# A hybrid encoder step on one core: new order of the last output tiles, of the first loads, and of everything a planner places between them

## The chip, the cores and the metric

The kernel runs on 1 core of one Trainium2 chip. The metric is the device time of one execution in microseconds (us). The time before is the median of three runs.

## The reference, cut to what matters

One layer of a streaming encoder, for 512 rows of a prompt and 32 rows of a sample (544 rows together) of width 1024. All arithmetic is float32.

```python
z = _rmsnorm(x, g) @ w_in                       # 3880 columns, split into the inputs of three groups of heads
oa = band attention (group A, 6 heads x 64)     # own chunk and the 8 before it, relative-position bias
ob = sparse attention (group B, 6 heads x 64)   # an indexer (8 heads x 32, one key) picks the best keys of each row
om = attention into 256 memory rows (group M, 4 heads x 64)
o = jnp.concatenate([oa * jax.nn.silu(ga), ob * jax.nn.silu(gb), om * jax.nn.silu(gm)], axis=-1)
x = x + o @ w_out                               # 1024 x 1024
y = _rmsnorm(x, norm_final_g)                   # the final norm
```

The keys and values of all groups are outputs too; the sample rows attend into caches of 512 (A), 1024 (B) and 256 (M) rows as well.

## The kernel before

**Products.** Each float32 operand is split into a high and a low part (names with h and l: wh, wl, xTh, xTl, oBh, oBl). A product of two operands is three matmuls (wh with xTh, wl with xTh, wh with xTl) that add up in one PSUM bank. For weights, ACT makes wh from the raw columns and POOL or DVE makes wl = raw - wh; for x, ACT makes xTh and DVE makes xTl.

**Order.** Nothing is ordered by hand. All instructions are recorded by one helper (so nearly all rows of the trace have line L400). A planner, the class Line, keeps an estimated clock for each engine and for the DMA queue of SP; generators (one for each task, such as loading, splitting, attention, output) yield the estimated time at which they want to go on, and the planner lets the one go on that fits. What a DMA is taken to last is a rate in `op` (L249). A generator that needs a PSUM bank waits in `room` or asks `there` (L458 to 472) until the bank is, by the estimate, free for some margin. So the numbers in these places decide the order in which every engine gets its instructions:

```python
        d = (outs[0].size() * 4 / 330e3 if eng == "SP" else
             self.cost(eng, op, outs, ins, kw) * (1.0 if eng == "PE" else SLACK))
            t = sorted(pp.free(f"b{b}") for b in free_banks)[k - 1] + 0.7
```

**Start.** `x_load` (L800) issues on SP's queue the norm weights g_mix, and for each of 8 K tiles (128 rows of the 1024) the K tile of x transposed (xr, 128 x 544) and the 296 columns of w_in for the indexer (raw, 128 x 296). ACT and DVE split both, and `index_group` multiplies: 8 K tiles, for each three token tiles of 128 rows, for each three matmuls of 296 columns, that is 72 matmuls. When PE's clock is behind the time at which operands are estimated to be there, `warm` (L909) puts filler matmuls `idle<-ones` into the gap (float32, so each is two passes and counts as two in the trace), with LATER = 0.3 us added to the gap.

**Middle.** Projections of all other columns with weights in pieces of 128 x 384 to 768; the three attentions; the sample's attention, with matmuls on parts of the array (forms 128\*64, 128\*32, 64\*128 in the trace); the caches of the sample are loaded by SP.

**End.** The output projection, `out_part` (L1963), is done in two parts: the heads of A and part of M first, and the rest (list B: three heads pairs of B and one tile of M) last. Part B before goes through columns 0 to 511 for token tiles t0 to t3 and then through columns 512 to 1023 for t0 to t3, the last in two halves of 256. Each result is added to the rows of x (`residual`, tile xr), and `settle` makes the final norm: a sum of squares of each piece (ACT, the last piece on DVE), the adds of these sums (tile ss, on POOL), the power -1/2 (POOL), the products with that factor and with norm_final_g (gf; on ACT, POOL, DVE), and a DMA of the whole 128 x 1024 tile out.

Of the kernel before, what the change touches and what calls it, by code (L numbers as in the profile page):

```python
# [91 lines left out]
class Line:  # L92
# [139 lines left out]
    def op(self, eng, op, outs, ins, kw):  # L232
# [11 lines left out]
        for x in outs_:  # L244
            b = self.box(x)
            for (w, _), o in self.reads[x.tensor.name].items():
                if all(p[0] < q[1] and q[0] < p[1] for p, q in zip(w, b)):
                    deps.setdefault(o, False)
        d = (outs[0].size() * 4 / 330e3 if eng == "SP" else  # L249
             self.cost(eng, op, outs, ins, kw) * (1.0 if eng == "PE" else SLACK))  # L250
# [178 lines left out]
def hybrid_step(ctx: ExitStack, tc: tile.TileContext, a: dict):  # L429
# [28 lines left out]
    def room(k=1):  # L458

        yield from line.wait(lambda: len(free_banks) >= k)  # L460
        while True:
            t = sorted(pp.free(f"b{b}") for b in free_banks)[k - 1] + 0.7
            if t <= line.now():
                return
            yield t
            yield from line.wait(lambda: len(free_banks) >= k)
# [4 lines left out]
    def there(k):  # L471
        return k == 0 or len(free_banks) >= k and sorted(pp.free(f"b{b}") for b in free_banks)[k - 1] + 0.7 <= line.now()

# [326 lines left out]
    def x_load():  # L800

        c = len(x_raw)
        yield from ()
        t = (rp.tile([P, 2, N], F32, tag="xr", name="xr", bufs=3) if c < 3 else
             cp.tile([P, 2, N], F32, tag="gate1", name="xr"))
        if c % 2 == 0:
            firsts.append(cp.tile([P, 2, 2, 296], F32, tag=("q0", "gate0")[c // 2], name="raw"))
        raw = firsts[c // 2][:, c % 2]
        for kk in range(2):
            rows = slice((2 * c + kk) * P, (2 * c + kk + 1) * P)  # L810
            if c == kk == 0:
                DMA.dma_start(gT[0], a["norm_mix_g"])
            DMA.dma_start(t[:, kk, :], a["x_t"][rows, :])
            DMA.dma_start(raw[:, kk, :], w_in[rows, QI:QI + 296])
        raws.append(raw)
        x_raw.append(t)
# [92 lines left out]
    def warm(until):  # L909
        fill, line.warm = line.warm, None  # L910
        until += LATER if until - line.clk["PE"] > WARM else 0
        while until - line.clk["PE"] > WARM:
            PE.matmul(idle[:, 0:P], ones, ones, start=True, stop=True)
        line.warm = fill
# [1048 lines left out]
    def out_part(ks, c0, done, order, apart=()):  # L1963

        ws = []
        for t in order:
            halves = 2 if t in apart else 1
            n = 512 // halves
            for f0 in range(0, 512, n):
# [3 lines left out]
                for i, k in enumerate(ks):  # L1973
                    if i == len(ws):
                        ws.append(w_next(1 + i))
                    wh, wl = (w[:, 0, f0:f0 + n] for w in ws[i])
                    st, en = i == 0, i == len(ks) - 1
# [7 lines left out]
                    PE.matmul(o, h, wl, start=False, stop=en)  # L1985
                line.spawn(evict([acc], [1], lambda _, p, t=t, f0=f0, n=n: residual(t, p[:, 0:n], c0 + f0, n),
                                 lambda t=t, f0=f0, n=n: done(t, c0 + f0, n)))

    def residual(t, acc, c0, n):
        x = xr[t][:, c0:c0 + n]  # L1990
        V.tensor_tensor(x, acc[:, 0:n], x, op=ALU.add)

    for c0 in range(0, D, 512):
        line.run(out_part(AM, c0, lambda *_: None, range(NT)))

# [14 lines left out]
    line.spawn(final())  # L2010
    pieces = [0] * (NT + 1)

    def settle(t, c0, n):
# [6 lines left out]
        new, run, old = s_[:, 2 * j:2 * j + 1], s_[:, 2 * j + 1:2 * j + 2], s_[:, 2 * j - 1:2 * j]  # L2020
        last = t == NT - 1 and c0 + n == D
        yield line.at(x) - 0.2
        if last:
            V.tensor_tensor_reduce(sq[:rows, 0:n], in0=x, in1=x, scale=1.0 / D, scalar=0.0, op0=ALU.mult, op1=ALU.add,
                                   accum_out=new)
        else:
            A.activation(sq[:rows, 0:n], x, AF.Square, scale=D ** -0.5, accum_out=new)
        if j == 0 or t == NT - 2:
            G.tensor_tensor(x, x, gf[:rows, c0:c0 + n], op=ALU.mult)
        yield line.at(new) - 0.2  # L2030
        if c0 + n < D:
            if j == 0:
                V.tensor_scalar(run, new, EPS, None, op0=ALU.add)
            else:
                G.tensor_tensor(run, new, old, op=ALU.add)
            return
        G.tensor_tensor(run, new, old, op=ALU.add)
        G.tensor_tensor(run, run, nhalf[:rows], op=ALU.pow)
        yield line.at(run) - 0.2
        y = xr[t]  # L2040

        m = D if t == NT - 2 else 512
        A.activation(y[:rows, 0:m], y[:rows, 0:m], AF.Copy, scale=run)
        if m < D:
            V.scalar_tensor_tensor(y[:rows, m:D], y[:rows, m:D], run, gf[:rows, m:D], op0=ALU.mult, op1=ALU.mult)
        DMA.dma_start(a["y_prompt"][t * P:(t + 1) * P, :] if t < NT else a["y_sample"], y)

    for c0 in range(0, D, 512):
        line.run(out_part(B, c0, lambda t, c, n: line.spawn(settle(t, c, n)),
                          range(NT), (NT - 1,) if c0 else ()))  # L2050
    while line.tasks:
# [66 lines left out]
```

## Time and profile before

| what | us |
|---|---|
| median of 3 runs | 354.46 |
| the three runs | 354.28, 354.46, 355.96 |
| the profiled execution, own time | 354.01 |
| its span (first to last instruction) | 352.2 |
| PE busy | 343.6 (98% of the span) |
| DVE, ACT, POOL busy | 278.3, 221.2, 179.5 |

The span is what the trace shows; the execution's own time is 1.8 us more. Busy time is the union of an engine's instructions: matmuls overlap, so the start of one to the start of the next says what one costs.

### The profile page before, as it was taken

The page shows a single profiled execution, that of the slowest core. Times are in us where ns is not written, and L with a number is a line of the kernel's source. Part 1 is how long each engine was busy: PE and PEld are TensorE (multiplying, and loading weights), DVE is VectorE, ACT ScalarE, POOL GpSimd, SP SyncE. Part 2 cuts the span into 40 slices and gives each one's busy share as a digit, 9 for nine tenths or more (in the row PEclk, how much of TensorE's full clock was granted, in tenths as well). Part 3 has the DMA queues.
Part 4 walks back from the last instruction along what each step waited for, and adds up shares of the span by engine and source line. Part 5 has one row for each costly group of instructions (what it writes and reads, how often), then busy time and mean ns, then how long its engine had stood idle before and what let it go on. Part 6 is the DMA issues. An engine that isn't in the chain of part 4 may idle for free.

```text
span 352.2 us, 7548 instructions
## 1 busy us (share of the span) xinstructions
PE 343.6 (98%) x2744; PEld 299.6 (85%) x2744; DVE 278.3 (79%) x705; ACT 221.2 (63%) x528; POOL 179.5 (51%) x197
## 2 busy tenths in 40 slices
PE   8999999999999999999999999999999999999991
PEld 7979978999999988887998998999986767776781
DVE  3765988878999979998999727999996689776552
ACT  5756677997767776786765328414793368573453
POOL 2568094475475557274654484552382064316543
PEclk9999999999999999999999999999999999999997
DMA  7999352375548223252131341234273285200014
GB/s 234 308 372 355 98 180 61 106 203 150 149 128 292 62 62 112 56 154 86 47 91 45 92 144 42 56 87 145 63 293 128 64 271 186 81 2 2 0 54 200
DMA packets 39604, 46.31 MB, mean 131 GB/s; under 512 B 5360, under 2 KB 32624, under 8 KB 39568
## 3 DMA queue, kind: packets, MB, share of 16 engines
q1 hardware_dynamic: 39568, 45.85, 41.8%
q8 instruction: 21, 0.34, 0.4%
q14 instruction: 15, 0.12, 0.1%
HBM read 39.67 MB, written 6.16 MB: 130 GB/s over the span
## 4 chain that ended last, share of the span: by engine, by line
PE 95%; DMA 1%; POOL 1%; SPq 1%; DVE 1%; issue 0%; ACT 0%; POOLq 0%; DVEq 0%; ACTq 0%
PE bank L400 95%; DMA xr<-in_x_t_dram 1%; SPq L400 1%; DVE xr L400 0%; POOL xr L400 0%; POOL ss L400 0%; ACT sq L400 0%; POOLq L2106 0%; DVE wl L400 0%; DVEq L400 0%; ACTq L400 0%
## 5 line engine op out<-in xcount | busy, mean ns | idle before, releaser
L400 POOL TENSOR_TENSOR wl<-raw,wh 128x512 fp32r<-128x512 f32 (+1 forms) x69 | 105.4, 1537 | 80.0 <-ACT wh L400 73.9
L400 ACT ACTIVATE wh<-raw 128x512 fp32r<-128x512 f32 (+2 forms) x77 | 50.5, 660 | 31.6 <-PE bank L400 17.1
L400 PE MATMUL bank<-wh,xTh 128*128 128x384 f32 (+1 forms) x184 | 63.8, 347 | 0.0
L400 PE MATMUL bank<-wl,xTh 128*128 128x384 f32 (+1 forms) x184 | 61.8, 336 | 0.4 <-DVE wl L400 0.4
L400 PE MATMUL bank<-wh,xTl 128*128 128x384 f32 (+1 forms) x184 | 61.2, 332 | 0.0
L400 ACT ACTIVATE z<-z,st 128x384 f32<-128x384 f32 (+3 forms) x80 | 42.4, 549 | 22.9 <-DVE st L400 22.7
L400 PE MATMUL bank<-xTh,wh 128*128 128x272 f32 x208 | 46.1, 303 | 0.0
L400 PE MATMUL bank<-xTh,wl 128*128 128x272 f32 x208 | 43.0, 288 | 0.0
L400 PE MATMUL bank<-xTl,wh 128*128 128x272 f32 x208 | 42.9, 288 | 0.0
L400 PEld LDWEIGHTS bank<-wh,xTh 128*128 128x128 f32 x184 | 34.9, 189 | 2.7 <-issue 2.0
L400 PEld LDWEIGHTS bank<-wl,xTh 128*128 128x128 f32 x184 | 34.7, 189 | 1.0 <-DVE wl L400 0.7
L400 PEld LDWEIGHTS bank<-wh,xTl 128*128 128x128 f32 x184 | 34.8, 189 | 0.0
L400 PEld LDWEIGHTS bank<-xTh,wh 128*128 128x128 f32 x208 | 32.7, 189 | 2.0 <-issue 1.4
L400 PEld LDWEIGHTS bank<-xTl,wh 128*128 128x128 f32 x208 | 32.6, 188 | 0.0
L400 PEld LDWEIGHTS bank<-xTh,wl 128*128 128x128 f32 x208 | 32.5, 189 | 0.0
L400 DVE MAX8 m<-ysel 128x8 f32<-128x256 f32 (+2 forms) x48 | 26.4, 550 | 0.1
L400 DVE MATCH_REPLACE8 ysel<-m,ysel 128x256 f32<-128x256 f32 (+2 forms) x48 | 26.1, 543 | 0.0
L400 PE MATMUL bank<-ident,z 128*128 128x128 f32 (+1 forms) x162 | 25.2, 275 | 0.0
L400 PEld LDWEIGHTS bank<-ident,z 128*128 128x128 f32 (+1 forms) x162 | 18.5, 140 | 5.5 <-issue 2.5
L400 ACT ACTIVATE junkS<-ysS,bi 128x1056 int8<-128x1056 f32 x16 | 18.7, 1169 | 4.3 <-DVE bi L400 4.3
L400 ACT COPY z<-bank 128x384 f32<-128x384 f32 (+2 forms) x26 | 13.2, 511 | 9.6 <-PE bank L400 8.5
L400 POOL TENSOR_TENSOR oBl<-o,oBh 128x128 fp32r<-128x128 f32 (+1 forms) x9 | 5.2, 577 | 27.1 <-ACT oBh L400 27.1
(300 smaller groups left out, 803.9 us busy)
## 6 DMA issues: line engine op xcount, KB each, us to landing
raw<-in_w_in_dram SPq DMA_DIRECT2D x20, 384.0 KB, 3.4
raw<-in_w_in_dram SPq DMA_DIRECT2D x26, 256.0 KB, 3.0
raw<-in_w_out_dram SPq DMA_DIRECT2D x16, 256.0 KB, 3.9
xr<-in_x_t_dram SPq DMA_DIRECT2D x8, 272.0 KB, 4.4
nat<-in_x_prompt_dram SPq DMA_DIRECT2D x4, 512.0 KB, 8.1
raw<-in_w_mem_kv_dram SPq DMA_DIRECT2D x8, 256.0 KB, 2.9
xr<-in_x_prompt_dram SPq DMA_DIRECT2D x4, 512.0 KB, 3.4
out_dram<-xr SPq DMA_DIRECT2D x4, 512.0 KB, 2.6
```

The lines of the kernel that those rows point to most:

```text
L400: return fn(*args, **kw)
```

## The change

Four edits. (1) At the end, part B goes through t0, t1, t2 with columns 0 to 511, the same three with columns 512 to 1023, and then t3 with both, its last piece in two halves. The sum of squares of t3's last half is started from the sum so far (`scalar=old`, `accum_out=run`), so no add follows it; t2 is treated like t0 and t1, with only its columns 0 to 511 multiplied by gf on POOL. (2) At the start x's first K tile is issued ahead of g_mix, and from the second K tile on the index weights are issued ahead of x. (3) The planner takes a DMA's rate as 200e3 for the first 2.5 us of SP's clock and as 370e3 after, in place of 330e3, and a margin of 1.0 in place of 0.7 for banks. (4) `warm` adds LATER only up to 7.5 us of the estimate.

```diff
-        d = (outs[0].size() * 4 / 330e3 if eng == "SP" else
+        d = (outs[0].size() * 4 / (200e3 if self.clk["SP"] < 2.5 else 370e3) if eng == "SP" else
...
-            t = sorted(pp.free(f"b{b}") for b in free_banks)[k - 1] + 0.7
+            t = sorted(pp.free(f"b{b}") for b in free_banks)[k - 1] + 1.0
...
             if c == kk == 0:
+                DMA.dma_start(t[:, kk, :], a["x_t"][rows, :])
                 DMA.dma_start(gT[0], a["norm_mix_g"])
-            DMA.dma_start(t[:, kk, :], a["x_t"][rows, :])
             DMA.dma_start(raw[:, kk, :], w_in[rows, QI:QI + 296])
+            if c + kk > 0:
+                DMA.dma_start(t[:, kk, :], a["x_t"][rows, :])
...
-        until += LATER if until - line.clk["PE"] > WARM else 0
+        until += LATER if WARM < until - line.clk["PE"] and until < 7.5 else 0
...
-        last = t == NT - 1 and c0 + n == D
+        last = c0 + n == D
         yield line.at(x) - 0.2
-        if last:
-            V.tensor_tensor_reduce(sq[:rows, 0:n], in0=x, in1=x, scale=1.0 / D, scalar=0.0, op0=ALU.mult, op1=ALU.add,
-                                   accum_out=new)
+        if t == NT - 1 and last:
+
+            yield from line.wait(lambda: summed[t] == j)
+            V.tensor_tensor_reduce(sq[:rows, 0:n], in0=x, in1=x, scale=1.0 / D, scalar=old, op0=ALU.mult, op1=ALU.add,
+                                   accum_out=run)
         else:
             A.activation(sq[:rows, 0:n], x, AF.Square, scale=D ** -0.5, accum_out=new)
-        if j == 0 or t == NT - 2:
-            G.tensor_tensor(x, x, gf[:rows, c0:c0 + n], op=ALU.mult)
-        yield line.at(new) - 0.2
-        if c0 + n < D:
+            yield line.at(new) - 0.2
             if j == 0:
                 V.tensor_scalar(run, new, EPS, None, op0=ALU.add)
             else:
                 G.tensor_tensor(run, new, old, op=ALU.add)
+        summed[t] += 1
+        if j == 0:
+            G.tensor_tensor(x, x, gf[:rows, c0:c0 + n], op=ALU.mult)
+        if not last:
             return
-        G.tensor_tensor(run, new, old, op=ALU.add)
+        yield line.at(run) - 0.2
         G.tensor_tensor(run, run, nhalf[:rows], op=ALU.pow)
...
-        m = D if t == NT - 2 else 512
-        A.activation(y[:rows, 0:m], y[:rows, 0:m], AF.Copy, scale=run)
-        if m < D:
-            V.scalar_tensor_tensor(y[:rows, m:D], y[:rows, m:D], run, gf[:rows, m:D], op0=ALU.mult, op1=ALU.mult)
+        A.activation(y[:rows, 0:512], y[:rows, 0:512], AF.Copy, scale=run)
+        V.scalar_tensor_tensor(y[:rows, 512:D], y[:rows, 512:D], run, gf[:rows, 512:D], op0=ALU.mult, op1=ALU.mult)
...
-    for c0 in range(0, D, 512):
-        line.run(out_part(B, c0, lambda t, c, n: line.spawn(settle(t, c, n)),
-                          range(NT), (NT - 1,) if c0 else ()))
+    order = [(t, c) for t0, t1 in ((0, NT - 1), (NT - 1, NT)) for c in (0, 512) for t in range(t0, t1)]
+    line.run(out_part(B, (0, 512), lambda t, c, n: line.spawn(settle(t, c, n)), order, order[-1:]))
```

The numbers of edit (3) move rows on every engine, so the diff of the code alone doesn't tell the order. Three places of it follow.

The first instructions on PE, before (bank_113 takes the fillers, bank_137 to bank_139 are the three token tiles of the index group):

```order
L400 MATMUL bank_113<-ones_114 128x128 x10
L400 MATMUL bank_137<-wh_140,xTh0_81 128x296
L400 MATMUL bank_113<-ones_114 128x128
L400 MATMUL bank_137<-wl_141,xTh0_81 128x296
L400 MATMUL bank_137<-wh_140,xTl0_83 128x296
L400 MATMUL bank_138<-wh_140,xTh0_81 128x296
L400 MATMUL bank_138<-wl_141,xTh0_81 128x296
L400 MATMUL bank_138<-wh_140,xTl0_83 128x296
L400 MATMUL bank_139<-wh_140,xTh0_81 128x296
L400 MATMUL bank_139<-wl_141,xTh0_81 128x296
L400 MATMUL bank_139<-wh_140,xTl0_83 128x296
L400 MATMUL bank_137<-wh_140,xTh0_81 128x296
```

The same place after:

```order
L400 MATMUL bank_113<-ones_114 128x128 x11
L400 MATMUL bank_137<-wh_140,xTh0_81 128x296
L400 MATMUL bank_137<-wl_141,xTh0_81 128x296
L400 MATMUL bank_137<-wh_140,xTl0_83 128x296
L400 MATMUL bank_138<-wh_140,xTh0_81 128x296
L400 MATMUL bank_138<-wl_141,xTh0_81 128x296
L400 MATMUL bank_138<-wh_140,xTl0_83 128x296
L400 MATMUL bank_139<-wh_140,xTh0_81 128x296
L400 MATMUL bank_139<-wl_141,xTh0_81 128x296
L400 MATMUL bank_139<-wh_140,xTl0_83 128x296
L400 MATMUL bank_113<-ones_114 128x128
L400 MATMUL bank_137<-wh_140,xTh0_81 128x296
```

The filler that stood between the first and the second matmul stands ahead of the first; one stands behind the first K tile. Two rows further, after the wl matmul of the second K tile, three fillers stand after the change; the pairs of fillers that before stood behind the first matmul of K tiles 2 and 7 (counted from 0) are gone, and one filler stands in K tile 3.

The end of POOL's program, before, from the multiply of t3's first half (xr_3804) on; ss holds the sums of squares, nhalf the exponent:

```order
L400 TENSOR_TENSOR xr_3804<-xr_3804,gf 128x512
L400 TENSOR_TENSOR ss<-ss 128x1
L400 TENSOR_TENSOR ss<-ss,nhalf 128x1
L400 TENSOR_TENSOR ss<-ss 128x1
L400 TENSOR_TENSOR ss<-ss,nhalf 128x1
L400 TENSOR_TENSOR xr_3657<-xr_3657,gf 128x512
L400 TENSOR_TENSOR ss<-ss 128x1
L400 TENSOR_TENSOR ss<-ss,nhalf 128x1
L400 TENSOR_TENSOR ss<-ss 128x1 x2
L400 TENSOR_TENSOR ss<-ss,nhalf 128x1
```

The same place after; t3's rows are now xr_3815:

```order
L400 TENSOR_TENSOR ss<-ss 128x1
L400 TENSOR_TENSOR ss<-ss,nhalf 128x1
L400 TENSOR_TENSOR ss<-ss 128x1
L400 TENSOR_TENSOR ss<-ss,nhalf 128x1
L400 TENSOR_TENSOR xr_3815<-xr_3815,gf 128x512
L400 TENSOR_TENSOR ss<-ss 128x1
L400 TENSOR_TENSOR ss<-ss,nhalf 128x1
```

The multiply of xr_3657 (t2's second half) is gone, t2's add and power stand ahead of t3's multiply, and between the last add and the last power there is now one add fewer.

SP's queue in the last third of the program, before (raw: a weight tile of w_out, of which there are four places; cache: half of the sample's cached values of group B):

```order
L400 DMA xrS<-in_x_sample_dram 32x1024
L400 DMA xr_3804<-in_x_prompt_dram 128x1024
L400 DMA raw<-in_w_out_dram 128x512 x4
L400 DMA cache<-in_cache_b_v_dram 128x4x384 x2
L400 DMA raw<-in_w_out_dram 128x512 x8
L400 DMA gf<-in_norm_final_g_dram 128x1024
```

The same place after:

```order
L400 DMA xrS<-in_x_sample_dram 32x1024
L400 DMA xr_3815<-in_x_prompt_dram 128x1024
L400 DMA raw<-in_w_out_dram 128x512 x8
L400 DMA cache<-in_cache_b_v_dram 128x4x384 x2
L400 DMA raw<-in_w_out_dram 128x512 x4
L400 DMA gf<-in_norm_final_g_dram 128x1024
```

The two loads of the cache stand behind eight loads of w_out where they stood behind four.

## Rows read from the trace of the kernel before

**Rows 1.** The page, part 1: busy time, share of the span, instructions.
```profile
PE 343.6 (98%) x2744; PEld 299.6 (85%) x2744; DVE 278.3 (79%) x705; ACT 221.2 (63%) x528; POOL 179.5 (51%) x197
```
**Rows 2.** Waits of PE behind its first filler: what for, us in total, times, longest.
```profile
PE bank L400 <- DVE wl L400: 0.4, 1, 0.4
```
**Rows 3.** Timeline of PE, index group: start, duration, operation.
```profile
1.05 4.63 PE L400 MATMUL bank<-ones 128*128 128x128 f32 x20 [1.05 <-DVE ones L400]
5.33 0.59 PE L400 MATMUL bank<-wh,xTh 128*128 128x296 f32 x1
...
7.03 0.29 PE L400 MATMUL bank<-wl,xTh 128*128 128x296 f32 x1
...
8.44 0.40 PE L400 MATMUL bank<-wl,xTh 128*128 128x296 f32 x1 [0.43 <-DVE wl L400]
...
9.64 0.30 PE L400 MATMUL bank<-wh,xTh 128*128 128x296 f32 x1
...
11.31 0.30 PE L400 MATMUL bank<-wh,xTh 128*128 128x296 f32 x1
```
**Rows 4.** Timeline of PE, end of the index group.
```profile
16.32 0.60 PE L400 MATMUL bank<-ones 128*128 128x128 f32 x4
...
17.72 0.30 PE L400 MATMUL bank<-wh,xTl 128*128 128x296 f32 x1
```
**Rows 5.** Timeline of ACT and DVE: operands of the second K tile.
```profile
6.31 0.75 ACT L400 ACTIVATE xTh<-xr,g_mix 128x544 fp32r<-128x544 f32 x1 [1.06 <-DMA xr<-in_x_t_dram]
...
7.09 0.92 DVE L400 SCALAR_TENSOR_TENSOR xTl<-xr,g_mix,xTh 128x544 fp32r<-128x544 f32 x1 [0.99 <-ACT xTh L400]
```
**Rows 6.** Timeline of POOL and PE: the first wl of the weights after the index group.
```profile
16.71 3.85 POOL L400 TENSOR_TENSOR wl<-raw,wh 128x768 fp32r<-128x768 f32 x2 [1.80 <-ACT wh L400]
...
21.50 0.34 PE L400 MATMUL bank<-wl,xTh 128*128 128x384 f32 x1
```
**Rows 7.** Timeline of PE round 201 us: full array, half array, full array.
```profile
200.55 0.34 PE L400 MATMUL bank<-wl,xTh 128*128 128x384 f32 x1
200.82 1.09 PE L400 MATMUL bank<-z,va 128*64 128x128 f32 x16
201.84 0.44 PE L400 MATMUL bank<-wh,xTh 128*128 128x384 f32 x1
202.12 0.34 PE L400 MATMUL bank<-wh,xTl 128*128 128x384 f32 x1
202.30 0.34 PE L400 MATMUL bank<-wl,xTh 128*128 128x384 f32 x1
```
**Rows 8.** Timeline of PE and POOL from the last matmul on.
```profile
344.88 0.28 PE L400 MATMUL bank<-wl,oBh 128*128 128x256 f32 x1
...
346.02 0.50 POOL L400 TENSOR_TENSOR ss<-ss 128x1 f32<-128x1 f32 x2
346.60 0.55 POOL L400 TENSOR_TENSOR ss<-ss,nhalf 128x1 f32<-128x1 f32 x1
```
**Rows 9.** Output DMAs: landing of all four; issue of the last two; landing of the last.
```profile
DMA to landing us min/median/max: 2.6/2.6/3.2
...
L400 SPq DMA_DIRECT2D out_dram<-xr x2: 332/332/332, 347.3 to 348.0; - x2
...
DMA to landing us min/median/max: 3.2/3.2/3.2
```
**Rows 10.** The cached values: SP's queue, POOL, PE, and the loads' landing.
```profile
283.74 0.93 SPq L400 DMA_DIRECT2D cache<-in_cache_b_v_dram  x2
284.99 11.93 SPq L400 DMA_DIRECT2D raw<-in_w_out_dram  x8
...
285.17 3.79 POOL L400 TENSOR_TENSOR wl<-raw,wh 128x512 fp32r<-128x512 f32 x3 [0.95 <-ACT wh L400]
...
291.93 1.10 PE L400 MATMUL bank<-cache,ptS 128*32 128x64 f32 x64
...
DMA to landing us min/median/max: 4.8/6.2/7.6
```

More of the change, by code (lines that the diff above doesn't have):

```diff
@@ L471, in there @@
     def there(k):
-        return k == 0 or len(free_banks) >= k and sorted(pp.free(f"b{b}") for b in free_banks)[k - 1] + 0.7 <= line.now()
+        return k == 0 or len(free_banks) >= k and sorted(pp.free(f"b{b}") for b in free_banks)[k - 1] + 1.0 <= line.now()
     def divided(k, issue):
@@ L1963, in out_part @@
     def out_part(ks, c0, done, order, apart=()):
-        ws = []
-        for t in order:
-            halves = 2 if t in apart else 1
+        ws = {c: [] for c in c0}
+        got = 0
+        for t, c in order:
+            halves = 2 if (t, c) in apart else 1
             n = 512 // halves
@@ L1973, in out_part @@
                 for i, k in enumerate(ks):
-                    if i == len(ws):
-                        ws.append(w_next(1 + i))
-                    wh, wl = (w[:, 0, f0:f0 + n] for w in ws[i])
+                    if i == len(ws[c]):
+                        got += 1
+                        ws[c].append(w_next(got))
+                    wh, wl = (w[:, 0, f0:f0 + n] for w in ws[c][i])
                     st, en = i == 0, i == len(ks) - 1
@@ L1985, in out_part @@
                     PE.matmul(o, h, wl, start=False, stop=en)
-                line.spawn(evict([acc], [1], lambda _, p, t=t, f0=f0, n=n: residual(t, p[:, 0:n], c0 + f0, n),
-                                 lambda t=t, f0=f0, n=n: done(t, c0 + f0, n)))
+                line.spawn(evict([acc], [1], lambda _, p, t=t, f=c + f0, n=n: residual(t, p[:, 0:n], f, n),
+                                 lambda t=t, f=c + f0, n=n: done(t, f, n)))
     def residual(t, acc, c0, n):
@@ L1993, in hybrid_step @@
     for c0 in range(0, D, 512):
-        line.run(out_part(AM, c0, lambda *_: None, range(NT)))
+        line.run(out_part(AM, (c0,), lambda *_: None, [(t, c0) for t in range(NT)]))
     gf = sq = ss = None
@@ L2011, in hybrid_step @@
     pieces = [0] * (NT + 1)
+    summed = [0] * (NT + 1)
     def settle(t, c0, n):
```

## The prediction

> **What bounds the kernel now.** I read the page's busy times first: PE is busy for 343.6 of 352.2 us [rows 1], every other engine far less. Then PE's waits: behind its first filler it waits once, 0.4 us for a wl tile [rows 2]. So from the first real matmul at 5.33 [rows 3] to the last at 344.88 [rows 8] PE is never out of work, and time is the sum of three things: what lies ahead of PE's saturated stretch, the work in that stretch (matmuls, fillers, changes of array form), and the tail behind the last matmul, 352.2 - 345.2 = 7.0 us. A faster side engine gives nothing; an edit pays only if it shortens one of the three, and costs if it makes PE wait. The timeline is therefore read at both ends and at a form change in the middle, and then wherever the new order puts an operand later than it is now.
>
> **Start.** Before: 20 filler passes from 1.05 to the first matmul at 5.33, 4.28/20 = 0.214 each; five matmuls and one filler more to 7.03 [rows 3], so about 0.22 a matmul. From 11.31 to 16.32 there are 37 matmuls, 0.1354 each [rows 3, 4], 1.22 for a K tile of nine. The K tile from 9.64 to 11.31 took 1.67: its two fillers cost 0.45, so 0.22 one. The pair at 16.32 costs the same. The last matmul starts at 17.72 [rows 4], and the group ends at 17.86.
>
> After: eleven fillers ahead, so the first matmul moves to 5.33 + 0.43 = 5.76. Nine matmuls of K tile 0: six at 0.22 reach 7.03, three at 0.135 end at 7.45. One filler: 7.7. K tile 1: two matmuls, three fillers (six passes at the dense rate, some 0.55 to 0.65), 8.6; then seven matmuls to 9.58. Before, K tile 2 began at 9.64: no more than 0.06 is gained by then. From there six K tiles at 1.22 and one filler of 0.22 end at 17.12, against 17.86. The gain, **0.7**, is thus three fillers that are gone (0.67) and 0.06 at K tile 1.
>
> Is x there? The order on SP's queue makes raw land ahead of x in a pair, so it is xTl that comes last, not wl. Before, K tile 1's xTh began on ACT at 6.31, when its x had landed, and its xTl on DVE ended at 7.09 + 0.92 = 8.01 [rows 5], with wl behind it ending the wait at 8.44 [rows 2, 3]. After, one transfer of weights (296 columns where x has 544) lies ahead of x that did not; if x comes 0.45 later (one issue of SP, from the 0.93 for two in [rows 10]), xTl ends at 8.5, just under the 8.6 at which the fillers end. So that wait is covered by fillers; with that cover too short by 0.5 the gain falls to 0.2. If DVE is ahead of the estimate and PE stands on 0.22 for less long it rises to 1.1. Bounds 0.2 and 1.1; I take 0.7, in the middle.
>
> What is late next is the first wl of the weights that follow: POOL makes two from 16.71 to 20.56, so the first by 18.7, and PE uses it at 21.50 [rows 6]. PE 0.7 earlier still comes 2 us after it. The gain is kept.
>
> **Middle.** The planner's new rates and margin move rows on all engines but neither add nor remove a real matmul. What they change for a saturated PE is how often it changes between the full array and parts of it. Going from 200.55 into the 64-column form at 200.82 takes 0.27, and the first matmul back takes 0.28 (201.84 to 202.12), where like ones follow at 0.18 (202.12 to 202.30) [rows 7]. So each change costs 0.09 to 0.10. Counted over PE's whole program there are 113 changes before and 108 after: **0.5**. Bounds: 0, if other places repay it (forms of few columns are not all priced by these rows), and 0.7.
>
> One load moves against this. The two loads of the sample's cached values were issued at 283.74, behind four w_out tiles; their first use is at 291.93, with landings 4.8 and 7.6 after issue [rows 10], so the second landed at 284.2 + 7.6 = 291.8: on time by 0.1. After, four more w_out tiles stand ahead in SP's queue, and each needs one of four places, which POOL frees with a wl of 3.79/3 = 1.26. Before, the fourth of them ended at 285.17 + 3.79 = 288.96 (with 0.95 of waiting for ACT in it) [rows 10]. So the cache is issued at 288.0 to 289.0, some 5 us later. In the order after, its use stands some 2.9 us later than before (three groups of three 512-column matmuls and a score group more ahead of it), at 294.8 by the old clock, and the second half of it at about 295.3. Queued behind the loads stand four w_out tiles and gf, which nobody needs soon. The second half is issued half a microsecond behind the first. With the old landing, 7.6, it is there at 296.1 to 297.1; with the landing of the first, 4.8 (much of the traffic that stretched the second, the w_out tiles, has moved ahead), at 293.3 to 294.3. PE would wait 0 to 1.8. The middle of these bounds, 295.2, is just on time with nothing to spare; I take **-0.3**, a little on the late side, as SP's queue can only slip one way.
>
> **Tail.** Before, POOL does two adds, the second only to join t3's last piece: 346.02, 0.50 for two, then the power at 346.60 [rows 8]. Without the second, the power starts about 0.27 earlier (0.19 for an add and the hop behind it). DVE's reduction takes the sum as its scalar and is no longer. POOL's multiply of t3's first half stands ahead of one add and the power, but needs only t3's first piece, which PE now ends two half pieces ahead of the end. The other part: the last two 512 KB outputs are now issued at 347.3 and 348.0, and the last lands in 3.2, where those that go alone need 2.6 [rows 9]. In the new order t2's last piece is followed on PE by all of t3 and not by its second half alone, so t2's output leaves one 512-column piece earlier and the last output goes alone: 0.56. Together **0.83**; bounds 0.27 and 0.9.
>
> The Trainium skill has a rule against that second part: "DMA: Bandwidth & Descriptors", section "Anatomy of one DMA — SWDGE (gpsimd) path", gives about 2.0 us plus bytes over 436 GB/s for one transfer, which is 3.2 us for 512 KB even alone; it would leave 0.27 of the tail's gain. It is stated for another path of issue, and three of the four rows here stand at 2.6.
>
> DVE gets one product of 512 columns more near the end (t2) and POOL loses one; both are idle beside PE there. Sum: 0.7 + 0.5 - 0.3 + 0.83 = 1.7. From the profiled execution's 354.01 that gives 352.3; the median of the runs is 0.45 above it, so **352.7**. About 0.5% (1.8 us: below 352.7 or above 356.2) is what a measurement of this kernel can tell from no change, so the forecast stands on that edge.
>
> **Rivals.**
> - *The cache is in time*: the middle gives its 0.5 whole, and what PE does earlier elsewhere is kept. 354.46 - 2.0 = 352.4, with the upper bounds 351.3. For it: the landing may shrink with the traffic. Against: SP's queue is in order, and 0.1 of slack was all there was. 0.22.
> - *The start gives nothing*: x of K tile 1 is later than one issue and the waits come back. 353.4. For it: before, x of tile 1 was what ACT waited for [rows 5]. 0.12.
> - *The cache comes at its late bound*, or another operand of the new order does the same: 1.8 in place of 0.3, 354.2. 0.12.
> - *A transfer's price is fixed*, as by the page's rule: t2's leaving early shortens nothing, and the tail gives 0.27. By rows that is the maximum of 3.2 for the last output though it goes alone, 353.3. The rows with 2.6 speak against it. 0.05.
> - *Slower*: SP's queue slips as a whole. Each w_out tile ahead of the cache also waits for ACT's wh before POOL's wl; if POOL's four run as before but ACT serves attention first, as it did once for 0.95, three times over, the cache goes out 2 to 3 us later still. It decides from a wait of PE of 4 us (1.8 + 2.0 of gains): 356.5. 0.07.
>
> **How the numbers follow.** Forecast 0.42, within 352.1 to 353.3, about half of it under the bound. Faster: 0.22 and 0.23 of the forecast, 0.45, to which the others give nothing; slower 0.07; the rest, 0.48, is same. The range leaves out about one in ten on each side: below the upper bounds of all gains, 351.3, and above the late cache with a little to spare, 354.4.
>
> **What would show it.** In the profile after: the first matmul near 5.8, no wait behind it, the index group's end near 17.1; 72 matmuls and 15 or 16 filler rows. A wait of PE for cache, if any, near 294 and under 1 us. The power 0.85 after the last reduction's end in place of 1.1, and a last output of 2.6. A PE wait anywhere else of more than 0.5 us, above all for wl or for a bank in the middle, would make the forecast wrong, as would form changes that cost other than 0.1.

## The result, and the profile after

| | before | after |
|---|---|---|
| median, 6 runs each (us) | 355.18 | 357.44 |
| lowest to highest | 354.28 to 356.31 | 356.90 to 358.49 |
| ratio to before | | 1.0057, 95% interval 1.0037 to 1.0076 |
| profiled execution, own time / span | 354.01 / 352.2 | 358.00 / 356.2 |

The change makes the kernel 2.0 us slower (0.57%), where 1.7 faster was forecast. The two profiled executions lie 4.0 apart, twice as much as the medians' ratio gives: that of before was among its fastest, that of after among its slower ones. So the trace after shows where time went in one execution, and the medians of the experiments say what is lost as a rule.

The page after, part 1:

```profile
PE 346.6 (97%) x2746; PEld 301.3 (85%) x2746; DVE 280.7 (79%) x704; ACT 222.4 (62%) x530; POOL 173.6 (49%) x193
```

All waits of PE after (what for, us in total, times, longest):

```profile
PE bank L400 <- DVE stk L400: 1.6, 2, 1.1
PE bank L400 <- DVE ones L400: 1.1, 1, 1.1
PE bank L400 <- DMA keysB<-in_cache_b_k_dram: 0.3, 1, 0.3
PE bank L400 <- POOL wl L400: 0.2, 1, 0.2
```

Before, the only wait behind the first filler was one of 0.4 for wl [rows 2]. It is gone, and 1.6 us for stk stand in its place, with 0.2 and 0.3 further on. stk are the split operands of the indexer, which PE transposes. The timeline of PE after, from 39 us on (start, duration, operation, wait ahead of it):

```profile
39.47 0.79 PE L400 MATMUL bank<-identR,stk 32*128 32x32 f32 x8 [1.08 <-DVE stk L400]
...
42.17 0.72 PE L400 MATMUL bank<-identR,stk 128*128 128x128 f32 x4 [0.47 <-DVE stk L400]
...
44.86 2.79 PE L400 MATMUL bank<-raw,xF 128*32 128x384 f32 x16
```

and the busy time of each engine by stretch, after (length, then PE, PEld, DVE, ACT, POOL, granted clock, DMA share, GB/s), with one stretch of before below it:

```profile
35.00:40.00 5.00, 3.92 (x27) 3.63 (x25) 4.21 (x9) 2.23 (x7) 1.12 (x1) 1.00 0.67 170
40.00:45.00 5.00, 4.53 (x24) 3.58 (x26) 4.45 (x11) 5.00 (x11) 2.24 (x2) 0.62 0.10 22
45.00:50.00 5.00, 5.00 (x32) 2.78 (x31) 2.70 (x6) 2.83 (x7) 3.64 (x5) 0.70 0.57 157
...
41.20:48.00 6.80, 6.33 (x31) 3.31 (x30) 4.75 (x10) 4.92 (x10) 4.37 (x4) 0.50 0.14 48
```

```profile
40.00:45.00 5.00, 4.96 (x35) 4.76 (x34) 4.91 (x14) 4.97 (x12) 1.05 (x2) 1.00 0.03 13
```

Behind the waits the granted clock has means of 0.62 and 0.70 of full speed in two stretches of 5 us: it stands at its lower level, 0.50, from 41.2 to 48.0, and at 1.00 in the stretches ahead of that and behind it. There the sixteen sample matmuls at 44.86 take 2.79. The same ones took 1.50 before, by its timeline:

```profile
45.35 1.50 PE L400 MATMUL bank<-raw,xF 128*32 128x384 f32 x16
```

In this one execution the two waits and the low clock are enough for the whole delay of the last matmul, 4.85 (349.73 for 344.88). An estimate: PE is busy for 6.33 of those 6.8 us, half of which, 3.2, the full clock would have saved, and 1.6 of waits make it 4.8. The medians are only 2.0 apart, and the experiments ask what of this is lost as a rule.

DVE is what PE waits for, by the timelines of DVE and POOL after, with one row of DVE before below them:

```profile
34.02 2.32 DVE L400 TENSOR_SCALAR kaS<-kaS,rs 32x384 f32<-32x384 f32 x1
...
38.64 0.68 DVE L400 TENSOR_TENSOR stk<-rotS,stk 32x512 fp32r<-32x512 f32 x1 [0.69 <-ACT stk L400]
...
41.59 1.03 DVE L400 TENSOR_TENSOR stk<-rot,stk 128x256 fp32r<-128x256 f32 x2
...
34.29 1.83 POOL L400 TENSOR_TENSOR wl<-raw,wh 128x768 fp32r<-128x768 f32 x1
```

```profile
36.49 0.40 DVE L400 TENSOR_SCALAR kaS<-kaS,rs 32x384 f32<-32x384 f32 x1
```

The product kaS of 32 x 384 takes 2.32 us; it ends 0.2 behind POOL's wl (34.29 + 1.83 = 36.12). Before, with no product of POOL beside it, it took 0.40. The other runs divide in the same way: 2.32 or 2.33 in e2, e3, e5 and e13 and 4.72 in e12, each time beside one or two of POOL's wl and ending 0.2 behind the last, and 0.40 in the eleven others, where no wl runs beside it. So DVE was held up by POOL here for 1.9 us. Behind it on DVE stands the whole chain of the sample's indexer up to stk at 38.64, which ends at 39.3, while PE was ready at 38.4. Without the 1.9 it would have ended near 37.4, an estimate, and PE would not have waited there.

The start, in PE's timeline after:

```profile
5.76 0.59 PE L400 MATMUL bank<-wh,xTh 128*128 128x296 f32 x1
...
8.15 0.83 PE L400 MATMUL bank<-ones 128*128 128x128 f32 x6
8.73 0.39 PE L400 MATMUL bank<-wh,xTl 128*128 128x296 f32 x1
...
17.23 0.30 PE L400 MATMUL bank<-wh,xTl 128*128 128x296 f32 x1
...
18.92 2.46 PE L400 MATMUL bank<-raw,xF 128*32 128x384 f32 x16
...
21.31 0.44 PE L400 MATMUL bank<-wh,xTh 128*128 128x384 f32 x1
```

And the tail after: PE, DVE and POOL, then the landing of the four outputs:

```profile
349.73 0.28 PE L400 MATMUL bank<-wl,oBh 128*128 128x256 f32 x1
...
350.60 0.48 DVE L400 CUSTOM_DVE_ANT_0 sq<-xr,ss 128x256 f32<-128x256 f32 x1
...
351.17 0.55 POOL L400 TENSOR_TENSOR ss<-ss,nhalf 128x1 f32<-128x1 f32 x1 [0.90 <-DVE ss L400]
...
DMA to landing us min/median/max: 2.6/2.6/2.7
```

From the last matmul's start to the end of the span it is 356.2 - 349.73 = 6.5, against 352.2 - 344.88 = 7.3 [rows 8]. So the end gave what was forecast. The index group ended 0.5 earlier, near the forecast, but the first projection behind it starts 0.26 later than before, and the last matmul 4.85 later.

### The profile page after: what moved, and what is told of

Read it like the earlier page. It is cut to its first block, busy times and chain, and to the rows that moved or that the text cites. A ratio compares the mean times of both kernels' runs of the same rounds, so it can differ in the third digit from the quotient of the medians.

```text
span 356.2 us, 7567 instructions
## 1 busy us (share of the span) xinstructions
PE 346.6 (97%) x2746; PEld 301.3 (85%) x2746; DVE 280.7 (79%) x704; ACT 222.4 (62%) x530; POOL 173.6 (49%) x193
## 4 chain that ended last, share of the span: by engine, by line
PE 83%; DMA 9%; DVE 3%; SPq 2%; issue 1%; POOL 1%; ACT 0%; POOLq 0%; ACTq 0%
PE bank L400 83%; DMA nat<-in_x_prompt_dram 3%; DMA xr<-in_x_t_dram 3%; DMA raw<-in_w_in_dram 2%; SPq L400 2%; DMA keysB<-in_cache_b_k_dram 2%; DVE kaS L400 1%; DVE wsel L400 1%; DVE xr L400 0%; POOL wl L400 0%; DVE stk L400 0%; DVE mTl L400 0%; DVE rotS L400 0%; ACT sq L400 0%; ACT stk L400 0%
## 5 line engine op out<-in xcount | busy, mean ns | idle before, releaser
L400 POOL TENSOR_TENSOR wl<-raw,wh 128x512 fp32r<-128x512 f32 (+1 forms) x69 | 102.2, 1488 | 85.0 <-ACT wh L400 79.3
L400 ACT ACTIVATE z<-z,st 128x256 f32<-128x256 f32 (+3 forms) x81 | 42.6, 549 | 22.6 <-DVE st L400 22.5
L400 PE MATMUL bank<-ident,z 128*128 128x128 f32 (+1 forms) x162 | 24.4, 272 | 0.0
L400 DVE SCALAR_TENSOR_TENSOR ysel<-r,wI,ysel 128x256 f32<-128x256 f32 (+2 forms) x21 | 17.8, 847 | 7.0 <-ACT r L400 6.3
```

What stands on the lines that cost most here:

```text
L400: return fn(*args, **kw)
```

## Experiments

Each ratio is to the kernel before on the same chip. Two theories stand against each other. O: one mistake of order, the sample's indexer ahead of the prompt's, makes a wait, and the low clock behind it is the loss. P: the planner's new numbers make another plan for all engines, and that plan fits the chip worse in many places, so that behind each wait stands the next. The first four expectations call them W and M.

**e1: the end alone.** The diff is that of the end in the section on the change, from `out_part` on.

> The kernel before with the new end alone (order of the last tiles, the running sum); start, planner's numbers and fillers as before. Theory W (PE waits at 38 and 42 us for the sample's stk, and the low clock behind it, made the loss; the end is worth what the tail of the two traces shows, 7.2 against 6.3 behind the last matmul): 0.8 to 0.9 us faster than before, ratio 0.9975, PE's waits as before. Theory M (the loss is spread over the middle, in many small places) says the same of this run. Theory E (the new end itself costs, for t3 stands alone on PE): no gain or a loss.

Measured: 354.71, ratio 0.9990 (0.9973 to 1.0008). A gain of 0.8 lies inside the interval, none does too. In its profiled execution the part behind the last matmul is 353.6 - 347.05 = 6.5, so the end does what it should there. But that execution lost the gain to a wait that the profile before did not have, for rows of a cache, up to 267 us, where the order of both is still the same:

```profile
PE bank L400 <- DMA keysB<-in_cache_b_k_dram: 1.7, 1, 1.7
```

The three loads were issued at the same time within 0.3 us, and the slowest took 7.8 us to land here and 6.1 before. So such a wait can differ from execution to execution of one order (the two ran on different chips); it may be part of the spread of before too (353.8 to 357.5 over all its runs).

**e2: the sample's transposes later**, by the planner.

```diff
-        yield line.sure(qsS)
+        yield line.sure(qsS) + 3.0
```

> The changed kernel, with the planner told to ask for the sample's transposes of stk 3 us later, so that the prompt's stand first on PE. Nothing else is edited, though the planner may move rows behind it. Theory W: no wait of PE for stk, clock 1.00 in 40 to 50 us, 4 us less than the changed kernel: about 353.3, 1.8 under before. Theory M: the wait goes, but the time falls by no more than the 1.6 of the waits or less: 355.8 to 357.

Measured: 360.25, ratio 1.0156 (1.0120 to 1.0192). Neither theory had this. The planner moved rows everywhere behind the edit; PE waits 1.5 for stk still, now the prompt's, and 0.5 to 0.9 for six other operands, of which two are shown:

```profile
PE bank L400 <- DVE stk L400: 1.5, 1, 1.5
...
PE bank L400 <- DVE o L400: 0.9, 1, 0.9
PE bank L400 <- DVE st L400: 0.8, 1, 0.8
```

It was no clean test, since it changed the plan, and it was the first sign for P.

**e3: the waits filled**, all else of the changed kernel in place. The diff shows the fillers ahead of the sample's transposes; two fillers stand ahead of the prompt's in the same way.

```diff
         p = bank()
+        for _ in range(5):
+            nc.tensor.matmul(p[:, 0:P], ident, ident, start=True, stop=True)
         for h in range(8):
             PE.transpose(p[:, h * T:(h + 1) * T].bitcast(F32R), flat(qsS[0:T], h), identR[:T, :T])
```

> The changed kernel with filler matmuls put into the two waits for stk (5 ahead of the sample's transposes, 2 ahead of the prompt's; about 1.0 and 0.4 us at full clock), the order of all else unchanged. Theory W with the clock as the larger part: the waits turn into fillers, the granted clock stays 1.00 in 40 to 50 us, time falls by 2.3 to 2.8, to about 355, level with before. If only the waits count and the clock costs nothing: no change, 357.4.

Measured: 357.52, ratio 1.0070 (1.0041 to 1.0098), as the changed kernel. The clock did what was expected, 1.00 throughout:

```profile
40.00:45.00 5.00, 4.92 (x41) 3.92 (x44) 4.43 (x12) 5.00 (x12) 1.79 (x2) 1.00 0.26 74
45.00:50.00 5.00, 4.17 (x35) 3.38 (x26) 4.29 (x7) 3.92 (x9) 4.04 (x5) 1.00 0.50 142
```

and the median did not follow. In the last five microseconds shown PE is busy for 4.17 only: with the clock kept up it waits 0.8 for DVE's sums (ss) there, an operand that the changed kernel did not wait for. The profiled execution alone, 356.21, is 1.8 under that of the changed kernel, though PE waited 0.9 for w_in at 20 us, ahead of the edit; it is the second fastest of five, and that of the changed kernel the second slowest of six. All five runs of e3 have a mean granted clock of 0.998 or 0.999 and take 356.08 to 358.02. Of the changed kernel's six runs one has 0.998 and takes 357.21, the others 0.989 to 0.993 and 356.90 to 358.49. So the low clock is not what the change costs as a rule; by the two intervals some 0.8 us of it can still be the clock's. The waits themselves are not tested here, since the fillers take as long.

**e4: the old DMA rate** in the changed kernel (330e3).

> The changed kernel with the planner's old DMA rate of 330e3; new start, margin, fillers' rule and end stay. By its order the sample's transposes stand 17 rows later on PE than in the changed kernel. Theory W: no wait for stk, about 353 (gain of the end 0.85, of the start 0.3 to 0.7), 2 under before. Theory M, if the rate is not what spreads the loss: 356 to 357.

Measured: 356.78, ratio 1.0050 (1.0024 to 1.0076). No wait for stk, and no gain: PE waits 0.9 for the cache, 0.9 and 0.4 for ACT, and the clock falls here too (means of 0.93 and 0.73 from 40 to 50 us).

**e5: the prompt's indexer first** in the changed kernel.

```diff
-        for g in (index_sample(), index_prompt(), picks()):
+        for g in (index_prompt(), index_sample(), picks()):
```

> The changed kernel with one edit: the generator of the prompt's index is started ahead of the sample's, as it came to stand in the kernel before; DVE then makes the prompt's stk ahead of the sample's, and PE's transposes of the sample stand 25 rows later. Theory O (the new numbers let the sample's chain go first on DVE, PE asks for it 1.1 us too early, and wait and low clock are the loss): no wait for stk, clock 1.00 from 40 to 50 us, 353.5 to 354.5. Theory P (the new numbers make a plan that fits the chip worse in many places; take one wait away and the next one shows): 356 to 358, with other waits.

Measured: 365.82, ratio 1.0289 (1.0260 to 1.0318). The wait for stk is gone and the clock is 1.00 from 40 to 50 us; the kernel is 8 us slower than the changed one. The edit made another plan, as in e2, so it says what another plan costs and not what the wait for stk costs in the changed one. In its profiled execution PE waits some 6 us behind 80 us (1.5 the longest), and the part behind the last matmul is 364.9 - 352.60 = 12.3 and not 6.5: DVE still has sums of the sample's rows to make.

**e6: the sample's transposes too early**, in the kernel before (`line.sure(qsS) - 4.0`).

> The kernel before with one edit: the planner may ask for the sample's transposes 4 us earlier, so that they stand 32 rows earlier on PE, about where the changed kernel has them. Nothing of the change is in it. Theory O: PE waits about 2 us for stk near 37 us, the clock falls behind it, and the kernel is 3.5 to 5 us slower than before: 359. Theory P: the wait is there, but costs little more than itself, or less: 356 to 357.5.

Measured: 369.50, ratio 1.0388 (1.0352 to 1.0423). The wait for stk is there, 1.8 us, and explains little of 14. Both theories were far off in size. The edit moved rows everywhere behind it too: the part behind the last matmul is 368.2 - 355.20 = 13.0, with DVE at the sample's rows as in e5.

**e7: the plan of before, with the new ends.** The planner is told the old order of loads, SP issues the new one.

```diff
+            for o, i in ((g_,) if first else ()) + (x_, w_):
+                line.op("SP", "dma_start", [o], [i], {})
+            for o, i in (x_, g_, w_) if first else (w_, x_):
+                nc.sync.dma_start(o, i)
```

> The kernel before with the new end, and with SP's first loads issued in the new order while the planner is told the old one: by the programs' orders only SP's first rows and the end differ from the kernel before. It tells what the load order is worth at a fixed plan. The end gives 0.8 by its tail (0.3 measured alone). If the load order helps as forecast (the 0.43 us wait for wl goes and xTl is not later): 0.3 to 0.4 more, 354.2. If xTl comes later than wl did: nothing more or a loss of 0.3, 354.7 to 355.

Measured: 354.41, ratio 0.9978 (0.9955 to 1.0002). At one plan the new loads and the new end lose nothing. The wait for wl at the start stays (0.45 at 8.47 by its trace), so the order of the loads alone does not remove it. The changed kernel has both and stands at 1.0057, so what it has beyond them, another plan and other fillers, costs 0.8%, 2.8 us (some 1.7 to 3.9 by the two intervals). The fillers' part is small by their number: 32 passes in the changed kernel and 30 in e7.

**e8: the margin alone**, 1.0 for 0.7 in the kernel before.

> The kernel before with the margin for banks at 1.0 in place of 0.7, and nothing else. Its first 200 rows on PE are those of before. Theory O: the margin is not what makes the loss, 354.5 to 355.5. Theory P: any new number makes a plan with new waits behind 100 us, 356 or more.

Measured: 366.16, ratio 1.0294 (1.0266 to 1.0321). A single number, one part of edit (3), takes 10.5 us. Two waits of PE, behind 100 us, are the largest:

```profile
PE bank L400 <- DVE ql L400: 4.0, 1, 4.0
PE bank L400 <- ACT z L400: 2.8, 1, 2.8
```

**e9: the new numbers from 60 us on**, over e7 (`330e3 if self.clk["PE"] < 60 else 370e3`, and the margin in the same way).

> The kernel of e7 (new end and new load order, the plan of before), with the planner's new numbers (rate 370e3, margin 1.0) from 60 us of its clock on; up to there its rows are those of e7. If the loss of the changed kernel is its wait for stk at 38 us and what follows it (theory O): as e7, 0.2% under before, 354.5. If the new numbers make worse plans wherever they are used (theory P): 1 to 10 us slower than before, with waits of PE behind 60 us, as e8 had them.

Measured: 362.40, ratio 1.0183 (1.0164 to 1.0202). Up to 60 us nothing differs from e7, so all of the 7 us are lost behind the place that O blames. PE's waits behind 60 us come to 1.0 only, so waits as in e8 are not what costs here. Much of it is the tail, 360.1 - 348.45 = 11.7 where e7 has 6.5. PE has done its last matmul at 348.45, but DVE has sums of the sample's rows (xrS) left over from the new plan:

```profile
350.34 1.40 DVE L400 TENSOR_TENSOR xrS<-bank,xrS 32x512 f32<-32x512 f32 x2
...
352.43 2.13 DVE L400 TENSOR_TENSOR xrS<-bank,xrS 32x512 f32<-32x512 f32 x3
...
356.29 0.74 DVE L400 SCALAR_TENSOR_TENSOR xrS<-xrS,ss,gf 32x512 f32<-32x512 f32 x1 [1.67 <-POOL ss L400]
...
357.09 0.33 SPq L400 DMA_DIRECT2D out_dram<-xrS  x1
```

The sample's output leaves at 357.09, where before it had left at 337.5.

**e10 and e11: one wait in the kernel before, and the same one filled.** The tile slow is made by three powers on POOL.

```diff
+        for _ in range(3):
+            nc.gpsimd.tensor_tensor(slow, slow, nhalf, op=ALU.pow)
+        nc.tensor.matmul(p[0:1, 0:1], slow, slow, start=True, stop=True)
         for t in range(NT):
             PE.transpose(p[:, t * P:(t + 1) * P].bitcast(F32R), flat(kst, t), identR)
```

> The kernel before, its plan untouched, with one wait put in: PE may go on at the prompt's transposes of stk (35.8 us) only when POOL, idle there, has done three powers of 0.55 behind its wl that ends at 35.4, at about 37.2. So PE waits some 1.4 us, as long as the changed kernel's two waits for stk together. If the low clock behind a wait costs as in the changed kernel's trace: granted clock under 1.00 in 37 to 50 us and 3 to 4 us slower than before, ratio 1.010. If a wait costs itself alone: 1.4, ratio 1.004. If other engines give it back: under 0.7, ratio under 1.002.

> As e10, with seven filler matmuls (1.3 us) ahead of the wait, so that PE is busy in it. The clock then stays at 1.00 and the cost is the wait's own 1.4, ratio 1.004; the difference to e10 is what the clock takes. If e10 and e11 come out alike, the clock takes nothing that counts.

Measured: 1.0047 (1.0030 to 1.0064) and 1.0058 (1.0039 to 1.0077). In the profiled executions the wait came out at 1.0 and the clock stayed at 1.00 with and without fillers, so this pair does not price the clock. The rows of e10:

```profile
PE bank L1145 <- POOL slow L1144: 1.0, 1, 1.0
```

```profile
35.00:40.00 5.00, 3.98 (x26) 3.62 (x25) 4.25 (x10) 1.89 (x5) 2.61 (x5) 1.00 0.59 148
40.00:45.00 5.00, 5.00 (x33) 4.96 (x32) 3.94 (x12) 4.35 (x9) 0.88 (x2) 1.00 0.18 47
```

What it does price is a wait in a plan that is otherwise whole: 1.7 us (1.1 to 2.3) where the profiled execution, the fastest of seven, waits 1.0. Nothing is seen to be given back later.

**e12: the rates alone**, in the kernel before.

> The kernel before with the planner's two DMA rates (200e3, then 370e3) and nothing else. Theory P: another plan with waits of its own, 1 to 10 us slower. Theory O, if the rate makes the sample's chain too early: PE waits for stk near 40 us and 4 us are lost.

Measured: 360.50, ratio 1.0139 (1.0117 to 1.0161); no wait for stk, but for the cache (1.8) and ACT (1.6).

**e13: the changed kernel without its waits for stk.** The transposes read the identity in place of stk, so the indexer's scores are of other data; the rows and their order are the same.

```diff
-            PE.transpose(p[:, h * T:(h + 1) * T].bitcast(F32R), flat(qsS[0:T], h), identR[:T, :T])
+            line.op("PE", "transpose", [o], [i, identR[:T, :T]], {})
+            nc.tensor.transpose(o, identR[0:T, :], identR[:T, :T])
```

> The changed kernel, its plan and order untouched, but the transposes of the sample's queries and of the prompt's keys read the identity, which is there at 33.7 us, and not stk (so the indexer's scores are of other data and the choice of keys is another; the work is the same). PE then has nothing to wait for at 38 and 42 us. If these waits and the clock behind them are the loss (theory O): 3 to 4 us under the changed kernel, 353.5 to 354.5, under before. If they are a part of it only and the rest of the plan loses too (theory P): 1 to 2 us under the changed kernel, 355.5 to 356.5.

Measured: 357.10, ratio 1.0042 (1.0023 to 1.0060): 0.5 us under the changed kernel, a difference inside the two intervals. The second of the two transposes now waits for the bank that it writes, which ACT has still to read (ka):

```profile
PE bank L400 <- DMA keysB<-in_cache_b_k_dram: 1.6, 1, 1.6
PE bank L1146 <- ACT ka L400: 1.6, 1, 1.6
```

```profile
40.00:45.00 5.00, 3.71 (x18) 2.50 (x22) 4.44 (x9) 5.00 (x11) 2.54 (x2) 0.67 0.03 7
```

One wait taken away at an unchanged order uncovered the next one, as long as the two for stk together, and the clock fell behind it as before, to a mean of 0.67. So this does not decide against O: the 1.6 us of waiting in that stretch were never taken away in the changed kernel's plan. The runs also show that the clock can count: the four of the twelve with a mean granted clock of 0.993 or more take 355.68 to 356.94, the others 356.22 to 358.95. In e2, e4 and e14 too the run with the highest clock is the fastest, by 1.3 to 2.4 us; these are single runs.

**e14 and e15: the numbers of before, slightly off**: the rate 335e3, and the margin 0.75.

> The kernel before with the planner's DMA rate at 335e3 in place of 330e3 (1.5%), and nothing else; its rows on PE differ in most places behind the first hundred. If the direction of the numbers is what costs: within 0.5 us of before. If the plan of before is one of few that fit, and any other loses (theory P in its strong form): 1 to 8 us slower.

> The kernel before with the margin for banks at 0.75 in place of 0.7, and nothing else. As e14: within 0.5 us of before if the size of the margin is what costs; 1 to 8 us slower if any other plan loses.

Measured: 360.39, ratio 1.0128 (1.0092 to 1.0164), and 366.45, ratio 1.0299 (1.0255 to 1.0342). It isn't the direction of the new numbers. Nor do the losses add up: the margin alone takes 10.5, the rates alone 5, and all edits together 2.0. Of the ten plans tried that are not the plan of before, none is as fast (ratios 1.0050 to 1.0388).

**e16: e7 without the four fillers in K tiles 2 and 7**, planned but not issued.

> The kernel of e7 (new end, new load order, plan of before) without the four fillers in K tiles 2 and 7: they are planned but not issued; by the trace of e7 the operands behind them are there already. All other rows stay. The index group then ends 0.9 us earlier, near 17.0. If the gain is kept: 0.9 under e7, ratio 0.9953 to before. If the loads of w_in that the sample's matmuls (raw with xF) need land no earlier (20.3 to 21 us in all traces so far), PE waits for them near 20 us and the ratio stays that of e7, 0.998.

Measured: 354.68, ratio 0.9973 (0.9956 to 0.9990). It is the one version that is measurably faster than before, by 1.0 us, and 0.8% faster than the changed kernel; that the fillers' part of it is real is not shown, since e7 lies inside its interval. In its profiled execution the index group's last matmul starts at 17.60, only 0.1 earlier than in e7 and not 0.9 (a second wait for wl, 0.46 at 11.66, took the place of one pair of fillers; the first, 0.45, is in e7 too), and at 21 us PE waits for w_in as e7 did (e16 first, e7 below):

```profile
21.06 0.84 PE L400 MATMUL bank<-raw,xF 128*32 128x384 f32 x4 [0.28 <-DMA raw<-in_w_in_dram]
21.83 0.44 PE L400 MATMUL bank<-wh,xTh 128*128 128x384 f32 x1
```

```profile
21.11 0.84 PE L400 MATMUL bank<-raw,xF 128*32 128x384 f32 x4 [0.18 <-DMA raw<-in_w_in_dram]
21.88 0.44 PE L400 MATMUL bank<-wh,xTh 128*128 128x384 f32 x1
```

## Why the prediction was wrong

**The step that failed** is the first sentence on the middle: that the new rates and margin change "how often it changes between the full array and parts of it", and else nothing, for a saturated PE. That PE is saturated was read from one execution of one plan. The ten other plans have waits of 1.5 us or more in their profiled executions, and the plan of before itself has 1.7 for one load in e1; so it is a property of a plan, and in part of an execution, and not of the kernel. The 113 and 108 changes of form were counted rightly and are beside the point. One late load was looked for and costed; the operands that DVE, ACT and POOL make were not followed through the new order, though DVE is busy for 4.91 of 5 us at 40 to 45 before, and the 1.9 us by which POOL held up kaS came with the new order. e8, e9, e12, e14 and e15 change the planner's numbers alone, or from 60 us on, and lose 4.6 to 10.6 us; e7 keeps the plan and loses nothing. So the size of this term was not +0.5 but -2.8, as the difference of the changed kernel to e7 (the fillers' rule is in it).

**Start: the mechanism was right, and the gain was not kept.** The last matmul of the index group starts at 17.23 and not at 17.72 [rows 4]: 0.5 in place of 0.7, as the three fillers in K tile 1 ended later than worked out (8.73 for 8.6) and the next matmul came slowly. But the first projection starts at 21.31, where it was 21.05 before:

```profile
21.05 0.44 PE L400 MATMUL bank<-wh,xTh 128*128 128x384 f32 x1
```

The step "PE 0.7 earlier still comes 2 us after it. The gain is kept" looked at POOL's wl only. Between lie the sample's matmuls, which read w_in as it lands: the sixteen at 18.92 take 2.46, where sixteen of that form took 1.50 at 45 us before. The two loads concerned, issue to landing, before and after:

```profile
L400 SPq DMA_DIRECT2D raw<-in_w_in_dram x2: 368/420/472, 13.7 to 14.1; - x2
...
DMA to landing us min/median/max: 5.6/5.9/6.1
```

```profile
DMA to landing us min/median/max: 6.0/6.3/6.5
```

They are issued 0.15 earlier (the first at 13.54 and not 13.69) and take 0.4 longer: they land 0.2 to 0.3 later. From 10 to 35 us the windows of both kernels show 290 to 380 GB/s and a DMA share of about 1.0; issuing earlier gave no earlier landing there. In e7 and e16 PE waits at the same place; that the loads swallow the gain of the start is shown for these three executions.

**The cache** was issued at 292.35, 8.6 later than before and not 5, and its use had moved to 301.12:

```profile
DMA to landing us min/median/max: 7.4/8.2/9.0
...
301.12 1.29 PE L400 MATMUL bank<-cache,ptS 128*32 128x64 f32 x64
```

The second half landed at 292.8 + 9.0 = 301.7, and no wait of PE shows for it: 0 in place of -0.3. The risk was real (e4 waits 0.9 there, e12 1.8), but here it cost nothing.

**Tail: right.** 0.85 by the traces where 0.83 was worked out. The power starts 0.57 behind the start of the last reduction, 0.85 before ([rows 8] and the reduction below), and all four outputs take 2.6 to 2.7. The sign that the prediction gives, 0.85 behind the reduction's end in place of 1.1, misreads the rows: 0.85 is what before has from its start.

```profile
345.75 0.42 DVE L400 CUSTOM_DVE_ANT_0 sq<-xr 128x256 f32<-128x256 f32 x1
```

The Trainium skill's rule ("DMA: Bandwidth & Descriptors", section "Anatomy of one DMA — SWDGE (gpsimd) path") would have 3.2 for the last one alone as well, an estimate for transfers that gpsimd issues. These are issued by SP, the measurement differs, and decides. By their times e1 and e7 can't tell 0.8 from 0.3.

**The rivals.** The one on the slower side had the sign and 7 in 100, but its place was SP's queue. The third allowed for "another operand of the new order" that comes late, at a price of 1.5 out of the gains, and the list of signs has a wait of more than 0.5 elsewhere: the 1.1 for stk is that sign. No rival said that the plan as a whole might be worse, which is what a change of a planner's numbers is first of all. One bound was added up wrongly: the upper bounds come to 2.7, which is 351.8 from the median before; 351.3 starts from the profiled execution.

What stays open: what in the changed kernel's plan makes up its 2.8 us in a usual execution. With the clock kept up nothing came back (e3, with some 0.8 left possible). The 1.6 us of waiting near 40 us are still a candidate for the larger part, as e13 only exchanged them for others. So of theory P the first half is shown, that another plan is what costs: by e7 against the changed kernel, and by the four runs that change the planner's numbers alone (e8, e12, e14, e15). That behind each wait stands the next is seen in e3 and e13 only.

## What to carry to other kernels

A change of the numbers by which a scheduler orders a program is a new program on every engine. Here its cost could not be worked out from the waits of the old trace, and a small step of a number was no small step of the time: 1.5% of a rate took 1.3%. To judge such a change, hold the order fixed and try its other parts at that order (as e7), and price the new plan by running it, over several executions: the one trace after was 4.0 us from the one before, the medians 2.0.

Where one engine is busy all the time in a well-fitted plan, ask of each stretch what would be next in line: taking the waits for stk away showed another of the same length (e13).

## What the runs showed that was not expected

The clock stood at 0.50 for 6.8 us behind two waits of 1.1 and 0.5 three us apart and had a mean of 0.67 over 5 us behind one of 1.6 (e13); it did not fall behind one of 1.0 (e10).

A DVE product of 32 x 384 that needs 0.40 took 2.32 while POOL's product of 1.83 ran beside it, in five kernels; in twelve with no such product beside it, it took 0.40. Which products hold each other up is not worked out here: before, one of DVE with 32 x 64 took 0.21 beside a wl of POOL.

One order up to there gave waits for the same cache load of 0 (before), 1.7 (e1) and 0 us (e7) in three executions, and another order 0.3 (the changed kernel) and 1.6 (e13). That is as much as the change moved the time.
